# Statistics of the middle norms by one ones-product each, a fifth folded FFN tile, two tiles normalised per product, and ties on GpSimd's products and the transposes

## The chip, the cores and the metric

The kernel runs on one core of a Trainium2 chip. The metric is the device time of one execution in microseconds (us); of several runs the median is taken. TensorE does the matrix products, VectorE, ScalarE and GpSimd the elementwise work, and SyncE issues the weight transfers.

## The reference

One decoder layer on 256 tokens, to which 16 meta tokens are prepended (272 in all). Width 2048, FFN width 5632, everything in float32. Cut to what the change touches:

```python
q, c_kv, q_idx, k_idx, w_idx, u = split_columns(h @ w_in[l])
c_kv = rms_norm(c_kv, kv_norm_g[l])                    # the latent norm, 256 features
...
mix = concat([attn_out, pool_out]) @ w_o[l]
h = layer_norm(ALPHA * h + mix, ln1_g[l], ln1_b[l])    # the middle norm
# conv_gated_ffn:
z = h @ w_up                                           # 2048 -> 2 * 5632
z = sum(pad(z)[:, j:j + T] * conv_w[j] for j in range(3)) + conv_b
a, g = split(z, 2);  f = (gelu(a) * g) @ w_down
h = layer_norm(ALPHA * h + f, ln2_g[l], ln2_b[l])
```

`layer_norm` takes mean and variance over the 2048 features of each token, `rms_norm` the mean square over its 256.

## The kernel before

Activations lie transposed: features on the 128 partitions, tokens in the columns (T = 272; from the middle norm on NQ = 258, since the convolution needs two tokens ahead of the 256). A vector of 2048 features is 16 tiles of 128. Every float32 product is made of two fp32r parts, high and low, of each operand: `product` (L201) runs per k-step three matmuls, high by high (L207), high by low activation (L208), low weight by high (L209), so 16 k-steps are 48 matmuls.

Weights come in tiles of 128 x 2048. `weights()` hands out the next tile and has the one two places ahead fetched: SyncE's queue loads it into `wraw` (three buffers), ScalarE copies each half of 1024 columns as the high part into `whl` (L162, three buffers), and VectorE subtracts it from the original for the low part (L163). In the text a *split* is this pair, a *half split* one half of it.

The order of the work on each engine is not written out: the code is walked through once, a scheduler gives every instruction its place in its engine's queue by the priority that follows from the order of the code and by when it estimates the operands to be ready, and on the chip each engine runs its queue in that order. An instruction that waits holds up all that stand behind it in its queue.

**The latent norm.** After the projection's first two products TensorE sums the squares of 256 features per token: `column_sums` (L253) takes the squares as the stationary operand, three blocks of tokens by two tiles, and leaves the sums with tokens on partitions. VectorE scales them, GpSimd raises them to the power −0.5, and `spread` (L259) multiplies the three columns by the identity, which writes the values as rows, equal on all partitions. VectorE applies the rows to the latent (`latent_norm`).

**The middle norm.** The W_o products (`output`) add each of 16 tiles to the residual. `about_k` (L641) then shifts the tile by a mean of the first four tiles, adds it and its square to running sums `s1`, `s2` on GpSimd (L650, L652), and makes from the tile, times the norm's gain, the high and low parts `fold`, with two more columns that hold gain and bias.

**The first FFN tiles.** f counts the 44 FFN tiles; each has two up-products, half 0 (gelu side) and half 1 (gate side), so up-product number 2f + half. The statistics of the middle norm are ready only some time into f = 0. So the first `FOLDED` = 4 tiles (eight products) multiply the weights with `fold`, which is not normalised yet, over 260 columns, and `unfold` (L731) mends the result: VectorE copies the two extra columns (L734) and multiplies by the row of 1/deviation (`rs`, L736), ScalarE makes the shift from the row `m2` (L738), GpSimd adds the two (L739). In the first product the statistics' own TensorE work is inserted: `deviation` (column sums of `s1` and `s2`) after k-step 7, `deviation_rows` (the spread of two rows, evicted by ScalarE) after k-step 14. From then on `normalise` makes the 16 normalised tiles `hp`, three after each folded product: GpSimd times `rs` (L708), VectorE plus `m2` (L709), ScalarE gain and bias (L710) and the high part (L712), VectorE the low part (L713). From f = 4 on products read `hp`.

After its two products a tile passes `conv` (ScalarE L726, VectorE L727 and L728, per half), and `gate`: Gelu on ScalarE (L743), times the gate side on VectorE (L744). Every second tile `forms` (L757) has GpSimd make sums of quarters of the pair (L761 to L764), and ScalarE and VectorE split them into high and low parts for the down-products, which use seven products for eight. At f = 4 and 5 VectorE transposes the 16 residual tiles in 32x32 blocks (L874), and from f = 6 on ScalarE's DMA queue moves the blocks (`residual`, 5 or 6 pieces per tile, 32 in all).

## Time and profile before

| what | value |
|---|---|
| median of 3 runs | 1037.93 us (1036.79 to 1038.07) |
| the profiled execution: time / span | 1038.06 / 1036.3 us |
| granted TensorE clock, mean | 0.997 |
| TensorE busy | 1024.8 us (99%), 7653 matmuls |
| VectorE / ScalarE / GpSimd busy | 885.7 (85%) / 621.1 (60%) / 210.1 us (20%) |
| DMA | 250.80 MB, 242 GB/s in the mean |
| first up-product starts | 302.56 us after the span's start |

The span is the stretch that the profiler sees of one execution; the time has 1.8 us more around it. TensorE is busy nearly all the time, so the table alone does not say what a microsecond less of another engine's work is worth. A row of the timeline is start, duration (us), engine, line, operation, output <- inputs, shapes and count; behind it in brackets stands a wait and what ended it. A matmul's printed duration (0.28) is longer than its distance to the next one (0.12), since matmuls are pipelined: for TensorE's cost starts are compared with starts. A row of the table of waits reads: engine and instruction, <- what ended its wait, then microseconds in all, how many waits, and the longest part.

### The profile page before, as it was taken

To read this page: it belongs to the slowest core of one execution; us is meant where nothing else is said; L and a number is where in the kernel's file an instruction comes from. 1 tells how busy PE (TensorE), PEld (TensorE's weight loads), DVE (VectorE), ACT (ScalarE), POOL (GpSimd) and SP (SyncE) were. 2 spreads that over 40 slices of the span, in tenths; PEclk is the share of its full clock that TensorE was granted. 3 is DMA by queue.
4 is the path that set the end of the run, shared out by engine and by line. 5 is a ranking of instruction groups with operands and counts; after the bars stand their busy time and mean duration, and the time that the engine had idled before them with its cause. 6 is when DMAs were issued, how large, how long until landed. Compare 5 with 4: busy or idle time off the path is not lost.

```text
span 1036.3 us, 19186 instructions
## 1 busy us (share of the span) xinstructions
PE 1024.8 (99%) x7653; PEld 974.0 (94%) x7653; DVE 885.7 (85%) x1374; ACT 621.1 (60%) x1001; POOL 210.1 (20%) x262
## 2 busy tenths in 40 slices
PE   9999999999999999999999999999999999999996
PEld 8998999999999999999999999999999999999975
DVE  6879568858879997899999999998999898999966
ACT  6666356655447865566566655565656666565655
POOL 1200014125436321212112021120211202110012
PEclk9999999999999999999999999999999999999998
DMA  9766543454552577998788787887888888888866
GB/s 322 256 220 225 194 166 105 141 195 162 203 192 94 194 233 219 276 320 277 266 293 277 289 279 264 293 278 265 297 264 300 274 290 275 266 277 289 292 200 160
DMA packets 59610, 250.80 MB, mean 242 GB/s; under 512 B 21718, under 2 KB 22400, under 8 KB 32384
## 3 DMA queue, kind: packets, MB, share of 16 engines
q1 hardware_dynamic: 34016, 229.37, 61.7%
q0 software_dynamic: 8320, 17.71, 8.8%
q10 hardware_dynamic: 17184, 2.49, 1.4%
q8 instruction: 60, 0.98, 0.4%
q14 instruction: 30, 0.25, 0.1%
HBM read 233.55 MB, written 3.16 MB: 228 GB/s over the span
## 4 chain that ended last, share of the span: by engine, by line
PE 89%; DVE 4%; issue 3%; DMA 1%; ACT 1%; POOL 1%; SPq 0%; DVEq 0%; POOLq 0%; ACTq 0%
PE mm L209 23%; PE mm L208 22%; PE mm L207 22%; PE at L797 6%; PE at L798 6%; PE at L796 6%; DMA wraw<-in_w_first 1%; DVE whl L163 1%; DVE x L709 1%; DVE hp L713 1%; PE at L367 0%; PE mm L490 0%; PE at L368 0%; POOL gb L888 0%; PE at L525 0%
## 5 line engine op out<-in xcount | busy, mean ns | idle before, releaser
L163 DVE TENSOR_TENSOR whl<-wraw,whl 128x1024 fp32r<-128x1024 f32 (+1 forms) x418 | 492.5, 1213 | 55.4 <-ACT whl L162 54.8
L162 ACT ACTIVATE whl<-wraw 128x1024 fp32r<-128x1024 f32 (+1 forms) x418 | 405.0, 1015 | 127.0 <-DVE wraw L158 35.8
L209 PE MATMUL mm<-hp,whl 128*128 128x258 f32 x1280 | 360.7, 282 | 0.0
L208 PE MATMUL mm<-hp,whl 128*128 128x258 f32 x1280 | 359.7, 281 | 0.0
L207 PE MATMUL mm<-hp,whl 128*128 128x258 f32 x1280 | 355.5, 278 | 0.0
L207 PEld LDWEIGHTS mm<-hp,whl 128*128 128x128 f32 x1280 | 240.7, 188 | 3.1
L208 PEld LDWEIGHTS mm<-hp,whl 128*128 128x128 f32 x1280 | 239.6, 187 | 3.0
L209 PEld LDWEIGHTS mm<-hp,whl 128*128 128x128 f32 x1280 | 240.2, 188 | 0.0
L207 PE MATMUL mm<-xp,whl 128*128 128x256 f32 (+5 forms) x384 | 110.9, 289 | 0.0
L208 PE MATMUL mm<-xp,whl 128*128 128x256 f32 (+5 forms) x384 | 108.5, 282 | 0.0
L209 PE MATMUL mm<-xp,whl 128*128 128x256 f32 (+5 forms) x384 | 108.0, 281 | 0.0
L797 PE MATMUL at<-whl,gp 128*128 128x512 f32 x212 | 83.7, 395 | 0.0
L796 PE MATMUL at<-whl,gp 128*128 128x512 f32 x212 | 83.7, 395 | 0.0
L798 PE MATMUL at<-whl,gp 128*128 128x512 f32 x212 | 83.4, 393 | 0.0
L208 PEld LDWEIGHTS mm<-xp,whl 128*128 128x128 f32 x384 | 72.3, 188 | 0.8 <-issue 0.5
L207 PEld LDWEIGHTS mm<-xp,whl 128*128 128x128 f32 x384 | 72.2, 188 | 0.6
L209 PEld LDWEIGHTS mm<-xp,whl 128*128 128x128 f32 x384 | 72.2, 188 | 0.3 <-DVE whl L163 0.2
L726 ACT ACTIVATE z<-mm,cv 128x256 f32<-128x256 f32 x40 | 22.7, 567 | 79.9 <-PE mm L209 79.0
L764 POOL TENSOR_TENSOR forms<-za 128x128 f32<-128x128 f32 x20 | 20.2, 1012 | 222.0 <-DVE za L744 207.5
L726 ACT ACTIVATE za<-mm,cv 128x256 f32<-128x256 f32 x40 | 22.6, 566 | 49.0 <-PE mm L209 49.0
L798 PEld LDWEIGHTS at<-whl,gp 128*128 128x128 f32 x212 | 39.8, 188 | 9.4
L796 PEld LDWEIGHTS at<-whl,gp 128*128 128x128 f32 x212 | 39.8, 188 | 8.2 <-DVE u L821 0.4
(305 smaller groups left out, 1842.8 us busy)
## 6 DMA issues: line engine op xcount, KB each, us to landing
wraw<-in_w_up SPq DMA_DIRECT2D x88, 1024.0 KB, 5.1
wraw<-in_w_down SPq DMA_DIRECT2D x80, 1024.0 KB, 6.4
wraw<-in_w_proj SPq DMA_DIRECT2D x24, 1024.0 KB, 5.1
wraw<-in_w_o SPq DMA_DIRECT2D x16, 1024.0 KB, 4.9
y<-v POOLq DMA_DIRECT2D x27, 256.0 KB, 8.8
y<-u POOLq DMA_DIRECT2D x18, 256.0 KB, 4.5
wraw<-in_w_first SPq DMA_DIRECT2D x8, 304.0 KB, 5.9
x<-in_xt SPq DMA_DIRECT2D x1, 2176.0 KB, 8.4
```

The costliest lines, as they stand in the source:

```text
L162: nc.scalar.activation(hl[:, 0, c], raw[:, c], AF.Copy)
L163: nc.vector.tensor_tensor(hl[:, 1, c], raw[:, c], hl[:, 0, c].bitcast(F32), op=ALU.subtract)
L207: nc.tensor.matmul(ps, wh, ah, start=n == 0, stop=False)
L208: nc.tensor.matmul(ps, wh, al, start=False, stop=False)
L209: nc.tensor.matmul(ps, wl, ah, start=False, stop=n == KT - 1)
L709: nc.vector.tensor_tensor(yd, yd, m2, op=ALU.add)
L713: nc.vector.tensor_tensor(a[:, 1, :NQ], yd, a[:, 0, :NQ].bitcast(F32), op=ALU.subtract)
L726: nc.scalar.activation(z, src[:, 2:NQ], AF.Identity, bias=col(C_B, j), scale=col(C_W, 3 * j + 2))
L764: nc.gpsimd.tensor_tensor(s[:, 3], a11, a21, op=ALU.subtract)
L796: nc.tensor.matmul(ps, a[:, 0, i], hl[:, 0, w], start=fresh, stop=False)
L797: nc.tensor.matmul(ps, a[:, 0, i], hl[:, 1, w], start=False, stop=False)
L798: nc.tensor.matmul(ps, a[:, 1, i], hl[:, 0, w], start=False, stop=last)
```

## The change

1. `column_sums` and `spread` go. `of_tokens` replaces the first: one fp32 product with a 128x128 matrix of ones as the stationary operand and the tile as the moving one, over 288 columns (TW; 272 or 258 tokens filled up with zeros), so that each partition holds all sums; VectorE transposes the result in 32x32 blocks, and column 0 of each block then holds the sums of 32 tokens: 9 columns (TB). `as_row` replaces the second: ScalarE copies each of the nine columns 32 times over, and VectorE transposes back. TensorE has no part in it. The small statistics are on 128x9 instead of 128x3, GpSimd's power among them. For the latent norm GpSimd first adds the squares of its two tiles, and one product does.
2. The middle norm's two ones-products come after k-step 8 of the first FFN product (before: sums after 7, spread after 14). `s1` and `s2` are tiles of their own with zeroed ends.
3. `FOLDED` is 5, and `normalise` is called for two tiles per folded product instead of three.
4. GpSimd's product in `normalise` is tied: it is issued after the last `unfold`'s sum on GpSimd. The transposes of f = 4 and 5 are tied behind the gate's product on VectorE.
5. A one-column Gelu on ScalarE at the first FFN product, whose result nobody reads, brings the table load forward.
6. The residual's 32 moves go 6, 6, 6, 6, 5, 3 over f = 6 to 11 instead of 6, 5, 5, 6, 5, 5.

TensorE's rows fall from 7473 to 7458, VectorE's from 1130 to 1123, ScalarE's from 758 to 757, and GpSimd's rise from 220 to 228; SyncE's are the same. The lines of the changed kernel are shifted: the weight split is L164 and L165, `product` L209 to L211, the ones-product L258, `normalise` L698 to L703, `unfold` L724 to L729, the gate's product L734, the transposes L864.

TensorE in the first FFN product, before (`at` is a PSUM tile, `mm` the product's):

```order
L209 MATMUL mm<-fold,whl 128x260
L253 MATMUL at<-ones,sums 128x64 x2
L253 MATMUL at<-ones,sums 2x64
L253 MATMUL at<-ones,sums 128x64 x2
L253 MATMUL at<-ones,sums 2x64
L207 MATMUL mm<-fold,whl 128x260
```

and after:

```order
L209 MATMUL mm<-fold,whl 128x260
L210 MATMUL mm<-fold,whl 128x260
L211 MATMUL mm<-fold,whl 128x260
L258 MATMUL at<-sums,ones 128x288 x2
L209 MATMUL mm<-fold,whl 128x260
```

Six matmuls of column sums became two over 288 columns, one k-step later; the spread's matmuls further down the product are gone.

GpSimd from the middle norm's power on, before:

```order
L693 TENSOR_TENSOR st<-st,half 128x3
L708 TENSOR_TENSOR x<-x,of_token 128x258 x16
L739 TENSOR_TENSOR u<-u,w 128x258 x2
L764 TENSOR_TENSOR forms<-za 128x128
L739 TENSOR_TENSOR u<-u,w 128x258 x2
L761 TENSOR_TENSOR forms<-za 128x128
L762 TENSOR_TENSOR forms<-forms,za 128x128
L763 TENSOR_TENSOR forms<-za,forms 128x128
```

and after:

```order
L686 TENSOR_TENSOR of_token<-of_token,half 128x9
L698 TENSOR_TENSOR x<-x,of_token 128x258 x4
L729 TENSOR_TENSOR u<-u,w 128x258 x2
L698 TENSOR_TENSOR x<-x,of_token 128x258 x4
L754 TENSOR_TENSOR forms<-za 128x128
L729 TENSOR_TENSOR u<-u,w 128x258 x2
L698 TENSOR_TENSOR x<-x,of_token 128x258 x4
L751 TENSOR_TENSOR forms<-za 128x128
L752 TENSOR_TENSOR forms<-forms,za 128x128
L753 TENSOR_TENSOR forms<-za,forms 128x128
L729 TENSOR_TENSOR u<-u,w 128x258 x2
L698 TENSOR_TENSOR x<-x,of_token 128x258 x4
```

The sixteen products that stood in one block now stand in four blocks of four, each behind the two `unfold` sums of a tile.

VectorE around the transposes, before (one of the ten places where they stand):

```order
L727 SCALAR_TENSOR_TENSOR za<-u,cv,za 128x256
L874 STREAM_TRANSPOSE x<-x 128x256
L728 SCALAR_TENSOR_TENSOR za<-u,cv,za 128x256
L874 STREAM_TRANSPOSE x<-x 128x256 x4
L734 COPY sc<-mm 128x2
L736 TENSOR_TENSOR u<-mm,of_token 128x258
L874 STREAM_TRANSPOSE x<-x 128x256 x2
L163 TENSOR_TENSOR whl<-wraw,whl 128x1024
L874 STREAM_TRANSPOSE x<-x 128x256
L163 TENSOR_TENSOR whl<-wraw,whl 128x1024
```

and after, around f = 4 and 5:

```order
L734 TENSOR_TENSOR za<-za,z 128x256
L864 STREAM_TRANSPOSE x<-x 128x256 x8
L717 SCALAR_TENSOR_TENSOR za<-mm,cv,za 128x256
L165 TENSOR_TENSOR whl<-wraw,whl 128x1024
L718 SCALAR_TENSOR_TENSOR za<-mm,cv,za 128x256
L165 TENSOR_TENSOR whl<-wraw,whl 128x1024
L717 SCALAR_TENSOR_TENSOR z<-mm,cv,z 128x256
L718 SCALAR_TENSOR_TENSOR z<-mm,cv,z 128x256
L165 TENSOR_TENSOR whl<-wraw,whl 128x1024
L734 TENSOR_TENSOR za<-za,z 128x256
L864 STREAM_TRANSPOSE x<-x 128x256 x8
L165 TENSOR_TENSOR whl<-wraw,whl 128x1024
```

The transposes moved from ten places among the steps of the first tiles into two blocks of eight, each behind a gate's product and ahead of a weight split.

The diff, cut to its core:

```diff
-FOLDED = 4
+FOLDED = 5
...
+TB = T // 32 + 1
+TW = 32 * TB
...
-    def column_sums(s, cuts, j, ps):
-        for i, (a, b) in enumerate(cuts):
-            for n, t in enumerate(s):
-                nc.tensor.matmul(ps[:b - a, 64 * (3 * j + i):64 * (3 * j + i) + 64], t[:, a:b], ones[:, :64],
-                                 start=n == 0, stop=n == len(s) - 1)
-    def spread(r, cuts, rb):
-        for i, (a, b) in enumerate(cuts):
-            nc.tensor.matmul(rb[:, a:b], r[:b - a, i:i + 1].to_broadcast([b - a, P]), ident[:b - a, :b - a],
-                             start=True, stop=True)
+    def blocks_of(t):
+        return t.rearrange("p (a b) -> p a b", b=32)
+    def of_tokens(o, s):
+        ps = small()
+        nc.tensor.matmul(ps[:, :TW], ones, s, start=True, stop=True)
+        nc.vector.transpose(o, ps[:, :TW])
+        return blocks_of(o)[:, :, 0]
+    def as_row(row, o, r):
+        nc.scalar.activation(blocks_of(o), r[:, :, None].to_broadcast([P, TB, 32]), AF.Copy)
+        nc.vector.transpose(row, o)
...
+    nc.gpsimd.tensor_tensor(sqs[0][:, :T], sqs[0][:, :T], sqs[1][:, :T], op=ALU.add)
...
     def latent_scale():
-        ps = small()
-        column_sums(sqs, cuts, 0, ps)
-        nc.vector.memset(v, 1.0)
-        for i, (a, b) in enumerate(cuts):
-            nc.vector.tensor_scalar(v[:b - a, i:i + 1], ps[:b - a, 64 * i:64 * i + 1], 1.0 / C, EPS,
-                                    op0=ALU.mult, op1=ALU.add)
+        nc.vector.tensor_scalar(v, of_tokens(sqs[1], sqs[0]), 1.0 / C, EPS, op0=ALU.mult, op1=ALU.add)
         nc.gpsimd.tensor_tensor(v, v, half, op=ALU.pow)
+        as_row(sqs[0], sqs[1], v)
...
     def deviation():
...
+        nc.vector.tensor_scalar_mul(mean1, of_tokens(s1w, s1w), 1.0 / D)
+        nc.vector.tensor_scalar(rstd1, of_tokens(s2w, s2w), 1.0 / D, EPS, op0=ALU.mult, op1=ALU.add)
+        nc.vector.tensor_tensor(square1, mean1, mean1, op=ALU.mult)
+        nc.vector.tensor_tensor(rstd1, rstd1, square1, op=ALU.subtract)
+        nc.gpsimd.tensor_tensor(rstd1, rstd1, half, op=ALU.pow)
+        nc.vector.scalar_tensor_tensor(less1, mean1, -1.0, rstd1, op0=ALU.mult, op1=ALU.mult)
+        as_row(rsw[:, :TW], s1w, rstd1)
+        as_row(m2w[:, :TW], s2w, less1)
...
-        nc.gpsimd.tensor_tensor(yd, yd, rs, op=ALU.mult)
+        with tc.issue_after(held["unfolded"]) if "unfolded" in held else ExitStack():
+            nc.gpsimd.tensor_tensor(yd, yd, rs, op=ALU.mult)
...
-        nc.gpsimd.tensor_tensor(u, u, w, op=ALU.add)
+        held["unfolded"] = nc.gpsimd.tensor_tensor(u, u, w, op=ALU.add).ins
...
-        nc.vector.tensor_tensor(za, za, zg, op=ALU.mult)
+        held["gated"] = nc.vector.tensor_tensor(za, za, zg, op=ALU.mult).ins
...
             if f + half_ == 0:
-                product(ps[:, :NE], hl, P, folded, 0, NE, k1=7)
+                nc.scalar.activation(rsw[:, TW:TW + 1], half[:, :1], AF.Gelu_apprx_tanh)
+                product(ps[:, :NE], hl, P, folded, 0, NE, k1=8)
                 deviation()
-                product(ps[:, :NE], hl, P, folded, 0, NE, k0=7, k1=14)
-                deviation_rows()
-                k = 14
+                k = 8
             product(ps[:, :NE], hl, P, folded, 0, NE, k0=k)
-            while len(h_parts) < min(KT, 3 * (2 * f + half_ + 1)):
+            while len(h_parts) < min(KT, 2 * (2 * f + half_ + 1)):
                 normalise(len(h_parts))
...
-        if f in (FOLDED, FOLDED + 1):
-            for m in range(8 * (f - FOLDED), 8 * (f - FOLDED) + 8):
-                nc.vector.transpose(y[:, m, NM:], y[:, m, NM:])
-        if FOLDED + 2 <= f < FOLDED + 8:
-            for _ in range((6, 5, 5)[f % 3]):
+        if f in (4, 5):
+            for m in range(8 * (f - 4), 8 * (f - 4) + 8):
+                with tc.issue_after(held["gated"]):
+                    nc.vector.transpose(y[:, m, NM:], y[:, m, NM:])
+        if 6 <= f < 12:
+            for _ in range((6, 6, 6, 6, 5, 3)[f - 6]):
```

More of the change, by code (lines that the diff above doesn't have):

```diff
@@ L242, in tile_layer @@
     nc.vector.memset(ones, 1.0)
-    half = sb.tile([P, 3], F32, name="half")
+    half = sb.tile([P, TB], F32, name="half")
     nc.vector.memset(half, -0.5)
@@ L298, in tile_layer @@
         nc.scalar.activation(ct[:, j, :], ps[:, :T], AF.Copy)
-        sq = temp([P, T], "sq")
-        nc.scalar.activation(sq, ps[:, :T], AF.Square)
+        sq = temp([P, TW], "sq")
+        nc.scalar.activation(sq[:, :T], ps[:, :T], AF.Square)
         sqs.append(sq)
+    nc.gpsimd.memset(sqs[0][:, T:], 0.0)
+    nc.gpsimd.tensor_tensor(sqs[0][:, :T], sqs[0][:, :T], sqs[1][:, :T], op=ALU.add)
     widx = ap_.tile([P, 2, HI], F32, name="widx")
@@ L308, in tile_layer @@
     ctp = ap_.tile([P, 2, 2, T], F32R, name="ctp", tag="q")
-    cuts = ((0, P), (P, 2 * P), (2 * P, T))
-    v = sb.tile([P, 3], F32, name="rms_v")
+    v = ap_.tile([P, TB], F32, name="rms_v")
     def latent_scale():
-        ps = small()
-        column_sums(sqs, cuts, 0, ps)
-        nc.vector.memset(v, 1.0)
-        for i, (a, b) in enumerate(cuts):
-            nc.vector.tensor_scalar(v[:b - a, i:i + 1], ps[:b - a, 64 * i:64 * i + 1], 1.0 / C, EPS,
-                                    op0=ALU.mult, op1=ALU.add)
+        nc.vector.tensor_scalar(v, of_tokens(sqs[1], sqs[0]), 1.0 / C, EPS, op0=ALU.mult, op1=ALU.add)
         nc.gpsimd.tensor_tensor(v, v, half, op=ALU.pow)
+        as_row(sqs[0], sqs[1], v)
     def latent_norm():
-        rb = small()
-        spread(v, cuts, rb)
+        rb = sqs[0]
         for j in range(2):
@@ L634, in tile_layer @@
     acc = fp.tile([P, NQ], F32, name="acc", tag="acc", bufs=2)
-    sums = fp.tile([P, 2 * NQ], F32, name="sums", tag="u1", bufs=1)
-    s1, s2 = sums[:, :NQ], sums[:, NQ:]
-    of_token = fp.tile([P, 2 * NQ], F32, name="of_token", tag="u2", bufs=1)
-    rs, m2 = of_token[:, :NQ], of_token[:, NQ:]
+    s1w, s2w = (fp.tile([P, 2 * NE], F32, name="sums", tag="gp", bufs=19)[:, :TW] for _ in range(2))
+    s1, s2 = s1w[:, :NQ], s2w[:, :NQ]
+    rsw, m2w = (fp.tile([P, 2 * NQ], F32, name="of_token", tag=tag, bufs=1) for tag in ("u1", "u2"))
+    rs, m2 = rsw[:, :NQ], m2w[:, :NQ]
+    for t in (s1w, s2w):
+        nc.gpsimd.memset(t[:, NQ:], 0.0)
     folded = []
@@ L674, in tile_layer @@
                 about_k(len(folded))
-    cuts = ((0, P), (P, 2 * P), (2 * P, NQ))
-    st = fp.tile([P, 4, 3], F32, name="st", bufs=1)
-    nc.vector.memset(st, 1.0)
+    mean1, square1, rstd1, less1 = (rsw[:, TW + TB * j:TW + TB * j + TB] for j in range(4))
     def deviation():
-        ps = small()
-        column_sums([s1], cuts, 0, ps)
-        column_sums([s2], cuts, 1, ps)
-        for i, (a, b) in enumerate(cuts):
-            r = slice(0, b - a)
-            nc.vector.tensor_scalar_mul(st[r, 0, i:i + 1], ps[r, 64 * i:64 * i + 1], 1.0 / D)
-            nc.vector.tensor_scalar(st[r, 1, i:i + 1], ps[r, 64 * (3 + i):64 * (3 + i) + 1], 1.0 / D, EPS,
-                                    op0=ALU.mult, op1=ALU.add)
-        nc.vector.tensor_tensor(st[:, 2, :], st[:, 0, :], st[:, 0, :], op=ALU.mult)
-        nc.vector.tensor_tensor(st[:, 1, :2], st[:, 1, :2], st[:, 2, :2], op=ALU.subtract)
-        nc.vector.tensor_tensor(st[:2, 1, 2:], st[:2, 1, 2:], st[:2, 2, 2:], op=ALU.subtract)
-        nc.gpsimd.tensor_tensor(st[:, 2, :], st[:, 1, :], half, op=ALU.pow)
-        nc.vector.scalar_tensor_tensor(st[:, 3, :], st[:, 0, :], -1.0, st[:, 2, :], op0=ALU.mult, op1=ALU.mult)
-    def deviation_rows():
-        for j, dst in ((2, rs), (3, m2)):
-            ps = small()
-            spread(st[:, j, :], cuts, ps)
-            nc.scalar.activation(dst, ps[:, :NQ], AF.Copy)
+        nc.vector.tensor_scalar_mul(mean1, of_tokens(s1w, s1w), 1.0 / D)
[6 more added lines that the diff above has]
+        as_row(m2w[:, :TW], s2w, less1)
     y2 = fp.tile([P, 2, D], F32, name="y2", bufs=1)
```

## The prediction

> **What bounds the kernel.** I read the page's busy shares first, then who waits for whom on TensorE, then TensorE's timeline around the edited lines, then VectorE's and GpSimd's.
>
> ```profile
> span 1036.3 us, 19186 instructions
> PE 1024.8 (99%) x7653; PEld 974.0 (94%) x7653; DVE 885.7 (85%) x1374; ACT 621.1 (60%) x1001; POOL 210.1 (20%) x262
> PE 89%; DVE 4%; issue 3%; DMA 1%; ACT 1%; POOL 1%; SPq 0%; DVEq 0%; POOLq 0%; ACTq 0%
> ```
>
> TensorE is nearly never idle and carries 89% of the chain that ended last, so an instruction that leaves TensorE's queue shortens the kernel by its own start-to-start time, unless TensorE then waits. The 4% of VectorE lie almost wholly in the first FFN tiles, where the change works. Three waits of TensorE stand there:
>
> ```profile
> PE mm L209 <- DVE whl L163: 1.1, 2, 0.6
> PE at L253 <- POOL sums L652: 0.2, 1, 0.2
> 329.53 0.28 PE L208 MATMUL mm<-fold,whl 128*128 128x260 f32 x1
> 330.27 0.39 PE L209 MATMUL mm<-fold,whl 128*128 128x260 f32 x1 [0.46 <-DVE whl L163]
> 330.50 0.28 PE L207 MATMUL mm<-fold,whl 128*128 128x260 f32 x1
> 341.79 0.28 PE L208 MATMUL mm<-fold,whl 128*128 128x260 f32 x1
> 342.66 0.39 PE L209 MATMUL mm<-fold,whl 128*128 128x260 f32 x1 [0.59 <-DVE whl L163]
> 342.88 0.28 PE L207 MATMUL mm<-fold,whl 128*128 128x260 f32 x1
> ```
>
> Undisturbed, matmuls of a product start 0.12 us apart. 329.53 to 330.50 is 0.97 for two steps, so 0.73 lost; 341.79 to 342.88 loses 0.85. Each time TensorE wants the low part of the weights of the next product, which VectorE splits late.
>
> **The change part by part.** (a) Statistics on TensorE. The inserted products, with the neighbours that show what they cost:
>
> ```profile
> 30.11 1.32 PE L253 MATMUL at<-ones,sq 128*128 128x64 f32 x12
> 31.59 0.28 PE L208 MATMUL mm<-xp,whl 128*128 128x256 f32 x1
> 38.08 0.92 PE L259 MATMUL at<-ident,rms_v 128*128 128x128 f32 x6
> 39.16 0.28 PE L208 MATMUL mm<-xp,whl 128*128 128x256 f32 x1
> 305.08 0.76 PE L253 MATMUL at<-ones,sums 128*128 128x64 f32 x6
> 307.08 0.28 PE L208 MATMUL mm<-fold,whl 128*128 128x260 f32 x1
> 309.48 1.86 PE L259 MATMUL at<-ident,st 128*128 128x128 f32 x12
> 311.50 0.28 PE L208 MATMUL mm<-fold,whl 128*128 128x260 f32 x1
> 239.94 0.60 PE L670 MATMUL at<-acc,ones 128*128 128x258 f32 x2
> 240.49 0.28 PE L208 MATMUL mm<-mixp,whl 128*128 128x258 f32 x1
> ```
>
> From the first row of each pair to the second lies the insertion and one ordinary matmul of 0.12. Removed: 31.59 − 30.11 − 0.12 = 1.36 (latent sums), 39.16 − 38.08 − 0.12 = 0.96 (latent spread), 307.08 − 305.08 − 0.12 = 1.88 (sums of the middle norm, with the wait for GpSimd in it), 311.50 − 309.48 − 0.12 = 1.90 (its spread): 6.10 us. Added: three ones-products over 288 columns. The one ones-product that stands in the trace, over 258 columns, costs 240.49 − 239.94 − 0.12 = 0.43; times 288/258 is 0.48, three are 1.44. GpSimd's last sum ends at 306.01 (304.39 + 1.62, below); the new pair stands after 8 instead of 7 k-steps, at about 305.4, and its second half would wait some 0.15. Between no wait and the 0.23 of before I take 0.15.
>
> (b) Fifth folded tile: 96 matmuls over 260 columns instead of 258, at 0.12 each: 96 × 0.12 × 2/258 = 0.09 us. Its two `unfold`s add per product one copy and one product on VectorE (0.41), one ACTIVATE and one GpSimd sum; that goes into the ledger under (d).
>
> (c) Latent norm's new steps beside TensorE: a GpSimd sum of 272, an ACTIVATE and two VectorE transposes of 288, all near 30 to 41 us.
>
> ```profile
> 40.54 0.79 DVE L328 TENSOR_TENSOR ctp<-kt,ctp 128x272 fp32r<-128x272 f32 x2
> L407 PE MATMUL at<-ctp,whl x16: 284/287/328, 79.1 to 87.0; 128*128 128x272 f32 x16
> ```
>
> The first reader of the latent comes at 79.1, 38 us after it was ready, so these cost nothing; without that cover, about 2 us once. The Gelu table, loaded at 329.09 for 1.28 us, moves into ScalarE's idle stretch:
>
> ```profile
> 329.09 1.28 ACT L743 ACT_TABLE_LOAD   x1
> 222.85 1.06 ACT L162 ACTIVATE whl<-wraw 128x1024 fp32r<-128x1024 f32 x1 [2.65 <-PE mm L209]
> ```
>
> ScalarE sits idle 2.65 us before 222.85, where the order now has the load: free. ScalarE also has little to lose at 329, since VectorE is the later one there.
>
> (d) The order of VectorE, ScalarE and GpSimd in f0 to f5. First, when statistics are ready:
>
> ```profile
> 302.56 0.28 PE L207 MATMUL mm<-fold,whl 128*128 128x260 f32 x1
> 304.39 1.62 POOL L652 TENSOR_TENSOR sums<-sums,sq 128x258 f32<-128x258 f32 x1
> 308.29 0.89 POOL L693 TENSOR_TENSOR st<-st,half 128x3 f32<-128x3 f32 x1 [2.28 <-DVE st L692]
> 310.90 13.87 POOL L708 TENSOR_TENSOR x<-x,of_token 128x258 f32<-128x258 f32 x16 [1.72 <-ACT of_token L700]
> L969 POOL TENSOR_TENSOR few<-few,half 128x1 f32<-128x1 f32 x1 | 0.6, 575 | 7.8 <-DVE few L952 7.8
> 311.87 3.70 DVE L709 TENSOR_TENSOR x<-x,of_token 128x258 f32<-128x258 f32 x5 [2.49 <-ACT of_token L700]
> ```
>
> The power takes 0.58 on one column and 0.89 on three, 0.16 a column, so about 1.8 on nine. Spread and its two evictions go; two ACTIVATEs and four transposes of 288 come (about 0.4 each). Counted from the sums, GpSimd's first product starts near 311.6 instead of 310.9 and VectorE's near 312.5 instead of 311.9, while TensorE is 1.88 + 1.90 − 0.96 − 0.15 = 2.7 ahead. VectorE so begins 3.3 us later against TensorE than before. What saves it is that each product now carries two tiles instead of three. VectorE's prices:
>
> ```profile
> 321.82 2.45 DVE L713 TENSOR_TENSOR hp<-x,hp 128x258 fp32r<-128x258 f32 x3
> 329.00 2.35 DVE L163 TENSOR_TENSOR whl<-wraw,whl 128x1024 fp32r<-128x1024 f32 x2
> 332.77 0.75 DVE L713 TENSOR_TENSOR hp<-x,hp 128x258 fp32r<-128x258 f32 x2
> 338.83 1.08 DVE L874 STREAM_TRANSPOSE x<-x 128x256 f32<-128x256 f32 x3
> 339.84 0.43 DVE L727 SCALAR_TENSOR_TENSOR za<-u,cv,za 128x256 f32<-128x256 f32 x1
> 340.20 0.48 DVE L727 SCALAR_TENSOR_TENSOR z<-u,cv,z 128x256 f32<-128x256 f32 x1
> 342.52 0.42 DVE L744 TENSOR_TENSOR za<-za,z 128x256 f32<-128x256 f32 x1
> ```
>
> Start to start: half a weight split 1.15, an hp, x, gate or transpose 0.34 to 0.36, a conv step 0.40. With GpSimd at work an hp takes 0.8. From 311.87 to 325.86 VectorE did 9 x, 5 hp, 2 splits and 2 unfolds, 7.9 us by the quiet prices, in 14.0: GpSimd's sixteen products cost it 6.1 us.
>
> Ledger up to the weights of product 9 (second half of f4), by the new order: 16 x, 15 hp, 14 half splits, 6 unfolds, 12 conv steps, 3 gates, 3 form splits: 5.4 + 5.1 + 16.1 + 2.5 + 4.8 + 1.0 + 1.0 = 35.9, and 6.1 for GpSimd: 42.0. From 312.5 this ends at 354.5, the first half at 353.3. TensorE's first product starts at 302.56; with the ones-products (1.1) and 48 × 0.12 = 5.76 a product, product 9 starts at 355.5: a margin of some 2 us, less the waits of a queue that runs in order (x behind GpSimd's tied groups). At product 11 ScalarE has `right<-forms` ahead of the weights; it waits for GpSimd's forms, which wait for f3's gate; there I find no margin. So the two stalls of before (1.58) go, and new ones of 0 to 5 us come; 5 if GpSimd's ten `u` sums and its forms disturb VectorE as the sixteen products did. The ledger is nearest the low end, and I take 1.2.
>
> (e) The sixteen transposes now stand as two blocks of eight, 8 × 0.36 = 2.9 us each, behind the gates of f4 and f5. Behind the first wait conv and weights of product 13, behind the second half the weights of product 14; ScalarE's first residual DMA waits for the second block too, and queued behind it are product 12's eviction and the weights of product 15. By the same ledger each has 1 to 3 us left; nothing is added to the sum.
>
> **Sum.** −6.10 + 1.44 + 0.15 + 0.09 − 1.58 + 1.2 = −4.8. The profiled execution took 1038.06 (its span 1036.3 and 1.8 around it), so 1033.3; the median of the runs, 1037.93, lies 0.1 lower. Forecast 1033.2.
>
> **Rivals.** First, VectorE stays the late engine.
>
> ```profile
> 312.00:367.80 55.80, 54.75 (x456) 54.33 (x455) 55.76 (x104) 41.42 (x74) 25.66 (x29) 1.00 0.41 136
> ```
>
> For it: after the window's length stand TensorE's matmuls, its weight loads and VectorE, which is busy 55.76 of 55.80 us and will begin later against TensorE. The Trainium skill's "GPSIMD Engine Reference", section "8. Key points", says that GpSimd shares its SBUF interfaces with VectorE and contends with two-input instructions; the trace agrees (hp 0.8 beside GpSimd, 0.34 alone). By that rule tying GpSimd's products later lowers nothing: the 6.1 us come back, beside the splits of products 4 to 8. Against: the ledger has them and still closes. New stalls of 3 to 6 us: 1034.9 to 1037.9, say 1036.4.
>
> Second, slower: the transposes' blocks. If VectorE reaches product 11 without any margin, each block delays a weight split by its full 2.9, and ScalarE's queue behind the first residual DMA (an eviction and two ACTIVATEs of 1.06) adds 2 more: 7.8. It decides once more than 6.0 + 2.1 is lost, so only with some product's stall on top: about 1040. Against: product 12 on carries no normalising, and needs 3.6 of VectorE's 5.76.
>
> Third, the change does not do what it says: TensorE only reaches the weights sooner and waits for DMA instead.
>
> ```profile
> 372.00:378.00 6.00, 6.00 (x54) 6.00 (x53) 5.93 (x11) 4.61 (x6) 1.29 (x1) 1.00 0.84 224
> ```
>
> For it: the DMA share (last but one) is 0.84 there. Against: of TensorE's waits between 300 and 380 us none is on a DMA, and here it is busy 6.00 of 6.00. That would give 1037.
>
> **Chances.** Forecast (new stalls 0 to 3): 0.72, 1031.9 to 1034.9. VectorE late: 0.16. DMA: 0.06. Slower: 0.06. 0.2% is 2.1 us, what a measurement can tell: below 1035.8 faster. The first case and half the second give 0.80; the rest of it and the third 0.14 the same; 0.06 slower. Range 1031.4 (no new stall, less half a microsecond of run spread) to 1037.0, which takes in most of the second case.
>
> **What would show it.** Right: ones-products over 288 columns at about 0.5 each and no spread; TensorE's waits for VectorE's weight splits under 3 us in all; VectorE no longer in the chain at 312 to 342. Wrong: waits of TensorE on `whl` at products 9 to 15, or behind the blocks of transposes; a power that takes much over 2 us; ScalarE idle behind its first residual DMA.

## The result and the profile after

The changed kernel is slower: 1052.1 us (median of 4 runs, 1048.28 to 1053.70) against 1037.61, ratio 1.0137 (95% interval 1.0121 to 1.0152). Forecast was 1033.2, range 1031.4 to 1037.0. The profiled execution took 1053.28 us, its span 1051.5, 15.2 more than before.

The page of the changed kernel: span, busy shares, and the chain that ended last by engine.

```profile
span 1051.5 us, 19129 instructions
PE 1026.7 (98%) x7617; PEld 973.1 (93%) x7617; DVE 885.2 (84%) x1375; ACT 622.0 (59%) x1005; POOL 211.8 (20%) x268
PE 76%; DVE 7%; issue 4%; ACT 4%; DMA 3%; POOL 3%; ACTq 1%; SPq 0%; POOLq 0%; DVEq 0%
```

No engine has over 2 us more work than before (VectorE 885.2 against 885.7, TensorE 1026.7 against 1024.8). TensorE's part of the chain fell from 89% to 76%, and VectorE, ScalarE, DMA and GpSimd took it: these are waits. TensorE's own, in us in all, times, longest:

```profile
PE at L787 <- DVE whl L165: 7.8, 3, 3.9
PE mm L211 <- DVE whl L165: 5.2, 7, 1.3
PE at L367 <- ACT rl L370: 0.6, 1, 0.6
PE at L367 <- DVE qi L393: 0.5, 1, 0.5
```

L787 is the low-weight matmul of the down-products: 7.8 us, in a stage of which the prediction says nothing. Where the time went is read by comparing when the same product starts in both traces. The windows below are cut at such places; after the length stand TensorE, its weight loads, VectorE, ScalarE and GpSimd, then granted clock, DMA share and GB/s. Before:

```profile
302.00:348.00 46.00, 44.72 (x365) 43.59 (x364) 41.41 (x81) 33.17 (x61) 24.89 (x28) 1.00 0.40 136
348.00:390.00 42.00, 42.00 (x358) 42.00 (x358) 39.65 (x70) 28.50 (x48) 10.00 (x12) 1.00 0.68 217
424.00:472.00 48.00, 48.00 (x350) 45.36 (x349) 44.94 (x60) 29.17 (x43) 11.80 (x12) 1.00 0.93 292
```

and after:

```profile
302.00:348.00 46.00, 45.93 (x378) 45.37 (x377) 37.60 (x73) 30.76 (x56) 25.04 (x24) 1.00 0.46 157
348.00:390.00 42.00, 36.95 (x296) 35.46 (x295) 35.82 (x69) 26.87 (x45) 12.39 (x17) 1.00 0.45 152
424.00:472.00 48.00, 40.24 (x256) 36.08 (x255) 36.64 (x51) 22.32 (x33) 4.42 (x6) 0.90 0.79 228
```

Up to 348 us TensorE did more matmuls than before (378 against 365). In the second window it does 62 fewer, in the third 94 fewer, and there VectorE too is idle longer than before and the granted clock is 0.90.

Start of the same product against the profile of before, in us (minus is ahead; products 2f + half, the down-products start behind product 16; product 87 is the last). Rows are runs told of below, one execution each. What an edit did is read from one column to the next: before_666653 edits nothing ahead of product 12 and still starts 0.71 ahead.

| run | product 0 | 1 | 7 | 14 | 18 | 24 | 87 |
|---|---|---|---|---|---|---|---|
| changed kernel | −1.10 | −3.56 | −5.11 | +2.27 | +2.69 | +15.15 | +15.14 |
| after_prep | −1.03 | −3.50 | −5.05 | +2.30 | +2.38 | +3.02 | +3.51 |
| before_666653 | −0.71 | −0.70 | −0.71 | −0.71 | −0.71 | +4.83 | +4.83 |
| turns_655 | −1.88 | −4.35 | −5.89 | −0.54 | +0.73 | +0.65 | +1.69 |
| stats_only | −2.09 | −4.56 | −0.96 | −0.95 | −0.94 | −1.02 | +1.56 |
| f5_3_tie | −1.99 | −4.45 | +1.90 | +2.16 | +2.16 | +2.09 | +3.60 |
| f4_3_tie | −2.11 | −4.57 | +1.95 | +1.96 | +1.97 | +1.89 | +1.89 |
| f4_2_tie | −2.39 | −4.85 | −6.41 | +2.72 | +2.73 | +2.66 | +2.65 |
| stats_noadd | −1.46 | −3.92 | −3.55 | −3.54 | −3.53 | −3.61 | −3.62 |
| f5_2_dve_prep | −2.05 | −4.52 | −6.07 | −2.41 | −2.10 | −2.15 | +1.90 |

So most of the gain that was forecast (6.0 us without new stalls) came, 5.1 us by product 7. It was lost twice over: 7.4 us in products 7 to 13 (the first loss), and 12.5 us between products 18 and 24 (the second).

**The first loss.** GpSimd, VectorE and TensorE of the changed kernel around product 8:

```profile
349.20 1.34 POOL L729 TENSOR_TENSOR u<-u,w 128x258 f32<-128x258 f32 x1 [2.54 <-ACT w L728]
350.50 2.81 POOL L698 TENSOR_TENSOR x<-x,of_token 128x258 f32<-128x258 f32 x4
```

```profile
348.73 1.21 DVE L165 TENSOR_TENSOR whl<-wraw,whl 128x1024 fp32r<-128x1024 f32 x1
351.17 1.64 DVE L699 TENSOR_TENSOR x<-x,of_token 128x258 f32<-128x258 f32 x2 [1.23 <-POOL x L698]
352.73 1.66 DVE L165 TENSOR_TENSOR whl<-wraw,whl 128x1024 fp32r<-128x1024 f32 x1
361.83 0.48 DVE L717 SCALAR_TENSOR_TENSOR za<-u,cv,za 128x256 f32<-128x256 f32 x1 [1.27 <-ACT za L716]
```

```profile
352.89 0.28 PE L210 MATMUL mm<-fold,whl 128*128 128x260 f32 x1
354.45 0.39 PE L211 MATMUL mm<-fold,whl 128*128 128x260 f32 x1 [1.28 <-DVE whl L165]
```

ScalarE's `w` releases GpSimd's `u`; the tied products stand behind it; VectorE's `x` waits for them, and behind `x` in VectorE's queue stands the half split that TensorE needs at 353. VectorE idles while TensorE waits for VectorE. From the first `x` to the second half of product 9's weights, and over the same length in the kernel before (VectorE is the third engine):

```profile
311.34:359.55 48.21, 45.54 (x374) 44.84 (x373) 41.57 (x77) 35.70 (x66) 24.31 (x25) 1.00 0.39 132
311.87:360.08 48.21, 47.16 (x392) 46.74 (x391) 48.17 (x87) 37.71 (x68) 24.88 (x27) 1.00 0.38 132
```

VectorE is idle 6.64 us in the changed kernel and 0.04 before. Six of the seven waits at L211, 5.1 us in the table of waits, make this loss of 7.4. A wait costs more than its entry there: the prediction's two stalls have 0.46 and 0.59 beside 0.73 and 0.85 lost.

**The second loss.** VectorE, SyncE's queue and TensorE:

```profile
419.56 0.43 DVE L734 TENSOR_TENSOR za<-za,z 128x256 f32<-128x256 f32 x1
426.30 0.69 DVE L156 TENSOR_TENSOR wraw<-wraw 128x512 f32<-128x512 f32 x1 [6.31 <-DMA wraw<-in_w_down]
426.91 3.49 DVE L165 TENSOR_TENSOR whl<-wraw,whl 128x1024 fp32r<-128x1024 f32 x3
```

```profile
418.17 0.33 SPq L151 DMA_DIRECT2D wraw<-in_w_down  x1
```

```profile
424.50 1.07 PE L786 MATMUL at<-whl,gp 128*128 128x512 f32 x4
428.19 0.79 PE L787 MATMUL at<-whl,gp 128*128 128x512 f32 x1 [2.61 <-DVE whl L165]
428.78 0.63 PE L788 MATMUL at<-whl,gp 128*128 128x512 f32 x1
429.20 0.63 PE L787 MATMUL at<-whl,gp 128*128 128x512 f32 x1
431.55 0.40 PE L788 MATMUL at<-whl,gp 128*128 128x512 f32 x1
431.78 0.28 PE L210 MATMUL mm<-hp,whl 128*128 128x258 f32 x1
```

L156 is the preparation that `fetch` does on VectorE for a down tile of kind A (L159 to L161: kind B), before its splits. VectorE stood 6.31 us at the preparation of a tile whose transfer was issued only at 418.17, while the splits of the tile that TensorE wanted at 425 stood behind it. In the kernel before, the same preparation waits 1.17 us:

```profile
418.99 0.69 DVE L154 TENSOR_TENSOR wraw<-wraw 128x512 f32<-128x512 f32 x1 [1.17 <-DMA wraw<-in_w_down]
```

The instruction order says why. After (5187 is the weight tile that TensorE needs, 5266 the next A tile, two later):

```
498 L156 TENSOR_TENSOR wraw_5266<-wraw_5266 128x512
499 L165 TENSOR_TENSOR whl_5188<-wraw_5187,whl_5188 128x1024 x2
```

Before:

```
501 L163 TENSOR_TENSOR whl_5188<-wraw_5187,whl_5188 128x1024
503 L163 TENSOR_TENSOR whl_5188<-wraw_5187,whl_5188 128x1024
504 L154 TENSOR_TENSOR wraw_5266<-wraw_5266 128x512
```

The changed kernel has three such inverted places, and the three waits of TensorE at L787 are at these three (from 425.6, 446.6 and 464.0 us). The diff touches neither line: the scheduler made this order in answer to other edits.

### The profile page after: what moved, and what is told of

Same layout as the page of the kernel before. It is cut to its first block, busy times and chain, and to the rows that moved or that the text cites. A ratio compares the mean times of both kernels' runs of the same rounds, so it can differ in the third digit from the quotient of the medians.

```text
span 1051.5 us, 19129 instructions
## 1 busy us (share of the span) xinstructions
PE 1026.7 (98%) x7617; PEld 973.1 (93%) x7617; DVE 885.2 (84%) x1375; ACT 622.0 (59%) x1005; POOL 211.8 (20%) x268
## 4 chain that ended last, share of the span: by engine, by line
PE 76%; DVE 7%; issue 4%; ACT 4%; DMA 3%; POOL 3%; ACTq 1%; SPq 0%; POOLq 0%; DVEq 0%
PE mm L211 19%; PE mm L210 19%; PE mm L209 18%; PE at L787 5%; PE at L788 5%; PE at L786 5%; DVE whl L165 3%; ACT whl L164 2%; DMA wraw<-in_w_down 2%; POOL u L729 1%; DMA wraw<-in_w_proj 1%; DVE x L699 1%; ACTq L710 1%; PE mm L276 1%; DVE x L864 1%
## 5 line engine op out<-in xcount | busy, mean ns | idle before, releaser
L165 DVE TENSOR_TENSOR whl<-wraw,whl 128x1024 fp32r<-128x1024 f32 (+1 forms) x418 | 491.6, 1210 | 51.2 <-ACT whl L164 50.5
L164 ACT ACTIVATE whl<-wraw 128x1024 fp32r<-128x1024 f32 (+1 forms) x418 | 404.4, 1014 | 126.9 <-issue 31.3
L211 PE MATMUL mm<-hp,whl 128*128 128x258 f32 x1248 | 352.8, 283 | 2.5 <-DVE whl L165 2.5
L210 PE MATMUL mm<-hp,whl 128*128 128x258 f32 x1248 | 351.3, 281 | 0.0
L209 PE MATMUL mm<-hp,whl 128*128 128x258 f32 x1248 | 347.1, 278 | 0.0
L209 PEld LDWEIGHTS mm<-hp,whl 128*128 128x128 f32 x1248 | 235.3, 189 | 3.2
L211 PEld LDWEIGHTS mm<-hp,whl 128*128 128x128 f32 x1248 | 234.7, 188 | 3.6 <-DVE whl L165 3.3
L210 PEld LDWEIGHTS mm<-hp,whl 128*128 128x128 f32 x1248 | 234.0, 187 | 3.2
L209 PE MATMUL mm<-xp,whl 128*128 128x256 f32 (+5 forms) x384 | 110.8, 289 | 0.0
L211 PE MATMUL mm<-xp,whl 128*128 128x256 f32 (+5 forms) x384 | 108.0, 281 | 0.0
L787 PE MATMUL at<-whl,gp 128*128 128x512 f32 x212 | 85.0, 401 | 2.6 <-DVE whl L165 2.6
L209 PEld LDWEIGHTS mm<-xp,whl 128*128 128x128 f32 x384 | 72.2, 188 | 0.5
L211 PEld LDWEIGHTS mm<-xp,whl 128*128 128x128 f32 x384 | 72.2, 188 | 0.3 <-DVE whl L165 0.2
L787 PEld LDWEIGHTS at<-whl,gp 128*128 128x128 f32 x212 | 40.5, 191 | 11.3 <-DVE whl L165 3.4
```

What stands on the lines that cost most here:

```text
L164: nc.scalar.activation(hl[:, 0, c], raw[:, c], AF.Copy)
L165: nc.vector.tensor_tensor(hl[:, 1, c], raw[:, c], hl[:, 0, c].bitcast(F32), op=ALU.subtract)
L209: nc.tensor.matmul(ps, wh, ah, start=n == 0, stop=False)
L210: nc.tensor.matmul(ps, wh, al, start=False, stop=False)
L211: nc.tensor.matmul(ps, wl, ah, start=False, stop=n == KT - 1)
L787: nc.tensor.matmul(ps, a[:, 0, i], hl[:, 1, w], start=False, stop=False)
```

## The experiments

| run | median us | ratio to before | 95% interval |
|---|---|---|---|
| changed kernel | 1052.1 | 1.0137 | 1.0121 to 1.0152 |
| untied_pool | 1053.94 | 1.0157 | 1.0139 to 1.0175 |
| untied_turns | 1049.94 | 1.0116 | 1.0099 to 1.0133 |
| untied_both | 1050.84 | 1.0126 | 1.0095 to 1.0156 |
| stats_only | 1038.69 | 1.0009 | 0.9991 to 1.0027 |
| after_prep | 1041.14 | 1.0036 | 1.0020 to 1.0051 |
| before_666653 | 1043.59 | 1.0052 | 1.0035 to 1.0069 |
| turns_655 | 1040.03 | 1.0024 | 1.0013 to 1.0035 |
| stats_prep | 1038.46 | 1.0011 | 1.0001 to 1.0022 |
| f4_3_tie | 1040.68 | 1.0038 | 1.0025 to 1.0052 |
| f4_2_tie | 1040.89 | 1.0033 | 1.0021 to 1.0045 |
| f5_3_tie | 1041.05 | 1.0040 | 1.0025 to 1.0055 |
| stats_noadd | 1034.50 | 0.9968 | 0.9955 to 0.9980 |
| stats_dve_prep | 1040.93 | 1.0032 | 1.0010 to 1.0055 |
| f5_2_dve_prep | 1041.44 | 1.0035 | 1.0017 to 1.0053 |
| f5_3_dve_prep | 1039.46 | 1.0017 | 1.0000 to 1.0034 |
| early5 | 1044.88 | 1.0071 | 1.0047 to 1.0095 |
| early6 | 1040.18 | 1.0026 | 1.0014 to 1.0038 |

### First: which edit

untied_pool, against the changed kernel:

```diff
-        with tc.issue_after(held["unfolded"]) if "unfolded" in held else ExitStack():
-            nc.gpsimd.tensor_tensor(yd, yd, rs, op=ALU.mult)
+        nc.gpsimd.tensor_tensor(yd, yd, rs, op=ALU.mult)
```

> The changed kernel without the tie on GpSimd's products: all sixteen stand in one block again, ahead of the unfold sums; the transposes stay in two blocks of eight. Theory A (VectorE's queue waits on GpSimd and ScalarE because the products were tied behind the unfold sums: VectorE idle 12.2 us between 312 and 400 against 2.5 before): most of the 7.4 us lost in products 8 to 13 comes back, TensorE enters the down-products with a lead of several us, and the 12.9 us lost at 424 to 470 do not happen: about 1035. Theory B (the tied transposes put the residual's moves some 20 us later, among the down weights, and that makes the second loss): 7 us come back, the second loss stays, about 1045. Theory C (the fifth folded tile itself, with its two more chains VectorE, GpSimd, ScalarE, VectorE): within 3 us of 1052.

untied_turns:

```diff
-                with tc.issue_after(held["gated"]):
-                    nc.vector.transpose(y[:, m, NM:], y[:, m, NM:])
+                nc.vector.transpose(y[:, m, NM:], y[:, m, NM:])
```

> The changed kernel without the tie on the transposes: they lie spread among the steps of the first tiles, from f = 0 on, and the residual's moves may start earlier. GpSimd's products stay tied. Theory A: the first loss stays or grows, because VectorE's waits stay and the transposes come on top of them; 1046 to 1056. Theory B: the second loss of 12.9 us goes, about 1039. Theory C: within 3 us of 1052.

untied_both makes both edits.

> The changed kernel without either tie: fifth folded tile, two tiles normalised per product and the new statistics stay. Theory A: about 1034, little beside the run without GpSimd's tie alone. Theory B: about 1034 as well, and clearly below that run (1045). Theory C: still 1046 or more.

stats_only makes both, and sets `FOLDED = 4`, three tiles per product and moves `(6, 5, 5)[f % 3]`.

> Only the new statistics (and the early Gelu table): four folded tiles, three tiles normalised per product, no ties, residual moves 6, 5, 5 as before. All theories: the removed TensorE work counts in full, -6.10 + 1.44 + 0.15 = -4.5 us, less the 1.5 us that TensorE lost new in the changed kernel's profile at 40 to 43 us, where the latent norm's new steps stand on VectorE and ScalarE: about 1034.5, if VectorE's later start against TensorE (3.3 us) costs nothing with three tiles per product; if it costs its full size at the splits of products 4 and 6, 1037 to 1038.

Measured: 1053.9, 1049.9, 1050.8 and 1038.7. Neither tie alone carries the loss, nor do both together, which refutes A and B as they stood; C seemed to be left. The tie on the transposes has a part in the first loss: without it products 7 to 13 lose 5.3 us (−5.99 to −0.69) instead of 7.4. But all three slow runs still have the moves 6, 6, 6, 6, 5, 3, and in their instruction order the same three inverted places, which stats_only has not. That gave theory D.

### Second: the inverted order

after_prep, in `fetch` of the changed kernel:

```diff
+        tie = tc.issue_after(behind["split"]) if kind in ("A", "B") else ExitStack()
+        with tie:
+            if kind == "A":
+                nc.vector.tensor_tensor(b12, b12, b11, op=ALU.subtract)
...
-            nc.vector.tensor_tensor(hl[:, 1, c], raw[:, c], hl[:, 0, c].bitcast(F32), op=ALU.subtract)
+            behind["split"] = nc.vector.tensor_tensor(hl[:, 1, c], raw[:, c], hl[:, 0, c].bitcast(F32),
+                                                      op=ALU.subtract).ins
```

> The changed kernel with one more tie: VectorE's preparation of a down-weight tile (kinds A and B, L156 and L159 to L161 of the changed kernel) is issued behind the splits of the tile fetched before it. Without the tie it stands, at three places of the changed kernel's queue, ahead of the splits of the tile two before, and so waits for a transfer that TensorE does not need yet: VectorE idle 15.3 us there against 4.0 before. Theory D (this order makes the second loss): the 12.9 us lost between 424 and 470 us go, 1039 (1037 to 1041). Theory E (the down weights' transfers are simply late, crowded by the residual's moves): nothing changes, 1048 or more.

before_666653, against the kernel before:

```diff
-        if FOLDED + 2 <= f < FOLDED + 8:
-            for _ in range((6, 5, 5)[f % 3]):
+        if 6 <= f < 12:
+            for _ in range((6, 6, 6, 6, 5, 3)[f - 6]):
```

> The kernel before, with only the residual's 32 moves spread 6, 6, 6, 6, 5, 3 over f = 6 to 11. Nothing else is edited, but the scheduler answers with two of the three inverted places in VectorE's queue (the preparation of a B tile ahead of the splits of the tile two before). Theory D: a loss at each of the two places, of the size of the 1.5 and 5.6 us seen there in the changed kernel, a few us less where the lead is larger: 1040 to 1045. Theory E: within 1 us of 1037.8, since transfers and their number stay the same.

turns_655 is untied_turns with `(6, 5, 5)[f % 3]`.

> The changed kernel without the tie on the transposes and with the moves 6, 5, 5 as before: fifth folded tile, two tiles per product and the tie on GpSimd's products stay. VectorE's queue has none of the three inverted places. Theory D: the second loss of 12.1 us in the run without the transposes' tie goes, the first (5.3 us in products 7 to 12) stays: 1037 to 1039. Theory E: within 3 us of that run's 1049.9.

stats_prep is stats_only with the tie of after_prep.

> Only the new statistics, with the tie of the down-weight preparation behind the splits of the tile fetched before. Theory D: the 2.5 us that the run with the statistics alone lost at 470 to 480 us go: 1036.2. Theory E: 1038.7 as there.

after_prep came to 1041.1: 11 us of the loss are gone with one tie. It moves the preparations and a few of their neighbours in VectorE's queue; in the trace's order of execution four instructions of ScalarE, one of GpSimd and one matmul also change places, and SyncE's transfers none. Its product 14 starts where the changed kernel's does (+2.30 and +2.27), its product 24 at +3.02 instead of +15.15. TensorE's waits in it:

```profile
PE mm L214 <- DVE whl L167: 5.3, 7, 1.3
PE at L370 <- ACT rl L373: 0.6, 1, 0.6
```

The waits of the first loss are unchanged (5.3 in 7), those on the splits of the down-weights are gone. before_666653 is the counter-proof: an edit of the counts alone, with the same number of transfers, costs the kernel before 0.52% (interval 0.35% to 0.69%). In its waits, and on its VectorE:

```profile
PE at L797 <- DVE whl L163: 3.8, 1, 3.8
```

```profile
455.76 0.69 DVE L157 TENSOR_TENSOR wraw<-wraw 128x512 f32<-128x512 f32 x1 [4.04 <-DMA wraw<-in_w_down]
456.37 4.09 DVE L163 TENSOR_TENSOR whl<-wraw,whl 128x1024 fp32r<-128x1024 f32 x4
```

One of its two inverted places cost 5.5 us (−0.71 to +4.83); at the other VectorE waited 1.1 us and TensorE not at all. turns_655 (1040.0) agrees to 1 us with D. Theory E is refuted: the second loss is VectorE's order. stats_prep's 1038.5 shows no gain over stats_only (1038.7). The 2.5 us that stats_only's profile lost near 470 us lie at another row of VectorE, which the tie does not touch:

```profile
471.12 0.69 DVE L793 SCALAR_TENSOR_TENSOR y<-y,v 128x512 f32<-128x512 f32 x1 [3.16 <-DMA y<-x]
```

VectorE waits there for the residual's last move, which lands at 471.0. In stats_prep's profile it lands at 469.6, and TensorE loses 0.3 us. This third loss comes back below.

### Third: the first loss

f4_3_tie is turns_655 with `FOLDED = 4` and three tiles per product; f4_2_tie has only `FOLDED = 4`; f5_3_tie only three tiles per product.

> New statistics, four folded tiles, three tiles normalised per product, GpSimd's products tied behind the unfold sums (blocks of 6, 6, 4), transposes untied, moves 6, 5, 5. VectorE's queue has none of the three inverted places. Against the run with the statistics alone only the tie is new: there 4.4 us were lost at products 4 and 5, where the weight split came late behind VectorE's x and hp beside GpSimd's sixteen products, and TensorE's matmuls after the wait came 0.22 instead of 0.12 us apart. Theory F (the fifth folded tile, with its two more chains from VectorE over GpSimd and ScalarE back to VectorE, makes the loss of 5 to 7 us in products 7 to 13): the tie saves the 4.4 us and little is lost later, 1033 to 1035. Theory G (two tiles per product instead of three, so that normalising runs on to product 9, makes it): the same 1033 to 1035. Theory H (the tie itself makes it, because VectorE's x waits behind GpSimd's group): 1037 to 1040.

> The same with two tiles normalised per product (blocks of 4, 4, 4, 4 on GpSimd), four folded tiles. Theory F: 1033 to 1035 again. Theory G: the loss is there, 1038 to 1040; it may be more, since product 8 needs the last hp at once. Theory H: 1037 to 1040.

> Five folded tiles with three tiles normalised per product, GpSimd's products tied, transposes untied, moves 6, 5, 5. None of the three inverted places. Theory F: the loss of products 7 to 13 stays, 1038 to 1040. Theory G: it goes, 1033 to 1035. Theory H: 1037 to 1040.

Measured 1040.7, 1040.9 and 1041.1: F and G are refuted, each of them had at least one run at 1033 to 1035. The fifth folded tile costs nothing that can be seen (f4_3_tie and f5_3_tie both lose 6.4 to 6.5 us in products 1 to 6 and next to nothing from there to 24). Tiles per product set only the place of the loss: three tiles lose it in products 4 to 6, two tiles in products 7 to 13. H, with 1037 to 1040, is nearest, but stats_only, without the tie, also lost 3.6 us by product 7, and untied_both, without either tie, 6.4 us by product 14 (−4.80 at product 1, +1.61), so the tie is not all of it.

Next, what VectorE has to do there. stats_noadd is stats_only without the line that adds the shift row:

```diff
         nc.gpsimd.tensor_tensor(yd, yd, rs, op=ALU.mult)
-        nc.vector.tensor_tensor(yd, yd, m2, op=ALU.add)
```

> The new statistics alone, and left out: the sixteen VectorE additions of the shift row (x plus m2) in normalise, so that the FFN input lacks that shift. VectorE has 16 instructions less in products 1 to 7, 5.6 us by their quiet price of 0.35 and more beside GpSimd. Theory W (VectorE's work between the statistics and product 8 sets when TensorE can go on, so what TensorE was spared there, it waits): the 3.6 us that the run with the statistics alone lost in products 4 to 8 go, 1034 to 1035. Theory X (ScalarE's queue or GpSimd's pace is what is late; TensorE's longest wait in that run, 1.9 us, was on ScalarE's half of the split): 1037 to 1039.

The three runs with `dve` in their name have `nc.vector` instead of `nc.gpsimd` in the first of these lines, without the tie on it, and the tie of after_prep: stats_dve_prep on stats_only, f5_2_dve_prep and f5_3_dve_prep on five folded tiles (two and three tiles per product, transposes untied, moves 6, 5, 5).

> The new statistics alone, with normalise's first product (x times 1/deviation) on VectorE instead of GpSimd, and the down-weight preparation tied behind the splits before it. VectorE has 16 instructions more (5.6 us), but no GpSimd beside it (6.1 us by the prediction's ledger) and no wait for it. Theory W: the two cancel, 1038 to 1039. Theory X with GpSimd's pace as the late one: 1034 to 1036.

> Five folded tiles, two tiles normalised per product, both of normalise's steps on VectorE, GpSimd's products and the transposes untied, moves 6, 5, 5, the down-weight preparation tied. Normalising is spread over eight products without a wait on GpSimd. Theory W: VectorE then needs about 2.1 (x, x, hp of two tiles) + 2.3 (split) + 0.4 (unfold) + 0.8 (conv) + 0.2 (gate) = 5.8 us a product against TensorE's 5.76, so that TensorE's gain of 4.5 stays up to product 9 and little is lost after it: 1034 to 1036. Theory X: the loss of 5 us in products 7 to 13 stays, 1038 to 1041.

> The same with three tiles per product. Theory W: VectorE needs 3.2 + 3.7 = 6.9 us a product until product 6, over TensorE's 5.76, so about 4 us are lost at products 4 to 6 and the gain is gone: 1037 to 1039. Theory X: as with two tiles, 1038 to 1041.

stats_noadd came to 1034.5, inside W's 1034 to 1035. Windows of stats_only and of stats_noadd over the same stretch:

```profile
312.00:330.00 18.00, 14.92 (x117) 14.49 (x116) 18.00 (x27) 11.80 (x24) 13.28 (x15) 0.96 0.17 59
```

```profile
312.00:330.00 18.00, 16.61 (x136) 16.19 (x135) 14.89 (x28) 13.14 (x26) 14.48 (x17) 1.00 0.17 60
```

In stats_only VectorE is busy 18.00 of 18.00 us while TensorE stands 3.1; without the additions VectorE has 3.1 to spare and TensorE stands 1.4. From product 1 to 8 stats_only loses 3.6 us and stats_noadd 0.4. So with the statistics alone it is this step on VectorE that takes the gain. Two things these runs do not separate from the sixteen instructions' work: one hop less in the chain, and another order, since the scheduler answered with transposes earlier on VectorE. The time itself fell inside W's range in part by luck. With the earlier transposes the residual's moves start at 353.8 instead of 369.0 us and end at 454.9 instead of 471.0, so that the third loss, 2.6 us in stats_only between product 24 and the last, is gone too; W had not counted on it.

Taking GpSimd out at about equal VectorE time gained nothing (stats_dve_prep, 1040.9). In its profile the two cancel as W had it, −1.35 at product 14 against −0.95 in stats_only; the miss is the third loss, 4.1 us between products 24 and 26. f5_3_dve_prep (1039.5, 0.5 over W's range and inside X's) loses 4.2 us in product 7 and 2.2 in the third loss. f5_2_dve_prep missed its 1034 to 1036, and the table shows where: TensorE kept 4.3 of its lead through product 12, but lost 1.9 in product 13 behind the transposes and 4.1 at 469 us:

```profile
470.21 0.69 DVE L796 SCALAR_TENSOR_TENSOR y<-y,v 128x512 f32<-128x512 f32 x1 [3.52 <-DMA y<-x]
```

VectorE waits for the last of the residual's moves to land, as in stats_only. In the kernel before, that move lands at 467.9 and the addition waits 0.3: with the moves 6, 5, 5 a TensorE that comes earlier has next to no slack there. The last two runs move these earlier, `(7, 7, 6, 6, 6)[f - 6]` for f = 6 to 10, and `(5, 5, 5, 5, 6, 6)[f - 5]` for 5 to 10.

> The kernel with five folded tiles, two tiles per product, both normalising steps on VectorE and the down-weight preparation tied, with the residual's 32 moves 7, 7, 6, 6, 6 over f = 6 to 10 instead of 6, 5, 5, 6, 5, 5 over 6 to 11. In that kernel's profile TensorE was 2.1 us ahead of the kernel before up to 468 us and then lost 4.1 at 469 to 475, where VectorE's first addition into the fourth quarter of the output rows waited 3.5 us for the last moves to land, ahead of the weight split that TensorE needed. Theory W with this third loss as a matter of the moves' end: 1041.4 - 4 = 1036 to 1037.5, with a narrower spread of the runs. Rival (the transfers crowd each other, and earlier moves make the down weights late instead): 1039 or more.

> The same with the moves 5, 5, 5, 5, 6, 6 from f = 5 to 10, one tile earlier. Theory W: 1035.5 to 1037.5 as in the run with 7, 7, 6, 6, 6, if ScalarE's first moves don't wait for the last transposes; if they do, up to 2 us more. Rival: 1039 or more.

Both missed (1044.9, runs from 1040.3, the profiled one, to 1049.4; and 1040.2). The wait on the last move is gone from the profile of early5 and down to 0.5 us in that of early6, but early6 loses 5 us around products 13 and 14, where TensorE waits 1.8 for ScalarE's split, and early5 loses its lead in pieces from product 17 on. Whether the later weights are then late through crowded transfers or through ScalarE's queue was not told apart. No version with all of the work beat the kernel before.

## Why the prediction was wrong

- **TensorE's terms held.** The middle norm's product 0 took 9.54 us before and 7.08 after, −2.46 against the −2.67 forecast. Its two ones-products over 288 columns, with the rows around them:

```profile
304.23 0.28 PE L211 MATMUL mm<-fold,whl 128*128 128x260 f32 x1
304.35 1.47 PE L258 MATMUL at<-sums,ones 128*128 128x288 f32 x4
305.44 0.50 PE L209 MATMUL mm<-fold,whl 128*128 128x260 f32 x1
305.77 0.28 PE L210 MATMUL mm<-fold,whl 128*128 128x260 f32 x1
```

  From 304.35 to 305.77, less one matmul of 0.12, is 1.30; 0.96 and a wait of 0.15 were forecast.
- **The latent part is within the spread.** Forecast −1.84 by product 0; the profile has −1.10, with two new waits of 0.5 and 0.6 at L367 in it. But the seventeen profiles with this latent part run from +0.01 to −2.39, with a median of −1.88, so 0.7 us cannot be put down to it. "These cost nothing" is neither shown nor refuted.
- **The old stalls went** (1.55 us between products 1 and 7, forecast 1.58), and no stall stands before product 8, as the ledger said.
- **The step that failed first is the term of 1.2 us for new stalls, bounds 0 to 5.** It was 7.4, in products 8 to 13. The ledger summed VectorE's work and closed at 354.5 us for the second half of product 9's weights; the trace has 359.55. The work was right, 41.57 us busy against 42.0 forecast, and it began at 311.34 instead of 312.5. What the ledger put at nothing is waiting: 6.64 us idle in between, 3.7 of it before `x` (GpSimd's tied groups), 1.6 before a conv step and 1.3 before a split of forms (both released by ScalarE). The text names "the waits of a queue that runs in order" and gives them no number. An end time worked out by a sum of work is a lower bound, and it was used as the estimate. The idle time is read from the trace; no run with all of the work removes it and keeps the gain.
- **The first rival had the right engine, with another reason.** VectorE was late: stats_only stands at 1038.7 where TensorE was spared 4.5 us, and 3.6 of that went on VectorE in products 1 to 8, 2.6 on the residual's last move. But in the changed kernel VectorE was late by waiting; GpSimd's contention, which the rival named, was in the ledger and came out there. The loss, 7.4, is above its 3 to 6. It was given 0.16.
- **The step that decided the sign is one that was not taken**, 12.5 us between products 18 and 24 that stand in the sum as nothing. The sum ends at product 15. The order of the instructions behind it was not compared, although the transposes' tie and the moves' new counts act on ScalarE and VectorE there. The inverted rows could be read before any run. What they cost could not: their price is a transfer's landing less the lead at that moment.
- **The rival on the slower side had the sign, by another cause.** Its first block does stand ahead of product 13's split, and TensorE loses 1.5 us there (products 13 to 14) against the 2.9 priced; behind the second block it loses nothing. Undoing their tie leaves 1049.9: the sign was luck.
- **DMA as the bound** fits neither loss: in the second the wait is on a transfer that TensorE did not need yet. A late transfer, the residual's last move, does make the third loss, which shows only in runs without the second.

## What to carry to other kernels

When a scheduler sets the order, an edit to counts or ties far from the critical line can invert two instructions on a full engine; compare the whole order, and above all look for work that waits on a later transfer standing ahead of work that is needed sooner. Time taken from the bounding engine is worth no more than the lead of the engine that feeds it: before pricing such a cut, follow that lead product by product to the place where it is smallest, and past the edited stage: here the landing of the residual's last move took 1.5 to 4.1 us near 470 us in five runs that had escaped the second loss. A tie that keeps a helper engine out of the way also makes every reader of its result wait, and that wait holds all that stands behind the reader.
